# One hybrid decoder layer on one core: an earlier load of decay sums, two more PSUM banks for output chunks, gate samples by pairs of heads, and a tail that uses TensorE in place of GpSimd

## The chip, the cores and the metric

The kernel runs as one launch on one core of a Trainium2 chip. The metric is the device time of one execution in microseconds (us). A core has TensorE for matrix products (PE in the profile; PEld is its loading of weights, which runs beside the products), VectorE (DVE), ScalarE (ACT), GpSimd (POOL), and SyncE (SP), which here only starts transfers. Transfers (DMA) are started from the instruction queue of SP, ACT or POOL, and a queue runs its instructions in order.

## The reference

One decoder layer for 256 prompt tokens and 64 sample tokens (8 sequences of 8), 320 in all, in float32. Model width 2048, gate width 2048 in 16 heads of 128, state-space part (SSD) 2048 wide in 32 heads of 64 and 4 groups, state 128, FFN width 5632.

```python
h = rms_norm(x)
a_u, a_v, z, xbc, dt = split(h @ w_in)
# gate: per head, 128-token chunks; samples are 8 tokens each
v = layer_norm(gelu(a_v));  s = tril(w_s[head]) @ v[chunk, head] + b_s
gate_out = gelu(a_u) * s
# SSD: conv + silu on xbc, then per group g of 8 heads
da_cs = cumsum(dt * a)
decay = exp(tril(da_cs[t] - da_cs[s]))
y = (C B^T * decay) (dt x) + exp(da_cs) (C state) + d * x      # and the new states
ssm_out = group_rms_norm(y * silu(z))
x = x + rms_norm(concat(gate_out, ssm_out) @ w_out)
f = (gelu(conv(h2 @ w_up)[:, :5632]) * conv(h2 @ w_up)[:, 5632:]) @ w_down,  h2 = rms_norm(x)
y = x + rms_norm(f)
```

Outputs are y, the new SSD states, the last rows of the two convolutions, and v of the last gate chunk.

## The kernel before, in words

Activations lie with features on the 128 partitions and all 320 tokens in the free dimension. Each weight matrix comes in slabs of 128x1024 float32 (512 KB). `slab` (L100) starts the load of a slab on SP (`wraw`, L117), ACT rounds it to fp32r (`whi`, L123), and DVE subtracts (`wlo`, L124); each of the three tiles has three buffers. `accumulate` (L131) then makes three matmuls of 320 columns per 128x128 block: `whi` with the high part of the activation (L134), `whi` with its low part (L135) and `wlo` with the high part (L136). A slab so needs its `whi` for the first product of a block and its `wlo` for the third.

PSUM has eight banks here. Four belong to the pool `mm`: results of `project` (columns of `w_in` or `w_ffn_up`, named `ps`) and of `chunk_out` (named `pd`: 512 rows of `w_out` or `w_down`, 16 blocks of 128 outputs, each added to `acc_mix` or `acc_ffn` by DVE at L247). The other four belong to the pool `misc`, for everything small. Both pools hand out their banks in turn.

The program is written as a chain of projections and output chunks, with generator tasks in between: every few slabs `tick` advances the task at the head of `bg` by one step. A step issues its instructions into the engines' queues at that place. The tile scheduler adds the waits, and may shift an instruction among those of its engine by priority, so the order on each engine is fixed before the run.

The places of the change:

- **Gate.** `layer_norm` (L772 ff) normalizes v by token, in `vt` (128 tokens x 3 token tiles x 2048; the third tile has the 64 samples on partitions 0 to 63, and the other half is set to zero). `gate_mix(g)` handles four heads in one step, or in two: for each head two matmuls for the prompt's two chunks (L806, 128 columns) and one for the samples (L807, 64 columns). The sample weights `wS` are made by DVE from `w8`. These products are plain float32: each stands as two records of TensorE in the profile.
- **SSD.** `ssd(g)` runs in 13 steps over the slabs around it. `load_sums(j)` (L898) loads `cs`, the running decay sums of a pair of heads j; `decays` (L1041 to L1051) makes the decay matrices in the same tile, and `products` (L1062) multiplies with them (`y_ps`), at steps 6 (pairs 0, 1) and 12 (pairs 2, 3). `cs` tiles come from a pool of three buffers, and the two halves of the fourth state, `st3` (L906), take two of the same buffers at the group's start. L877 loads the other states. At the end of a group SP stores `s` and `x` (L1118, L1119).
- **Chunks.** `chunk_out(w_out, 3)` to `chunk_out(w_out, 6)` (L1180 to L1200) each follow a projection whose last results go through a convolution (`heads_in`: `pad` from `ps` at L452 and L453 on DVE, then L457 on ACT and L459 on DVE) or through `z_evac`.
- **Tail.** After the last chunk the squares are summed by matmul (`tsum`, L1391 and L1394), and `rsqrt_by_root` (L274 to L281) gives one factor per token, `rs_r`. The result lies in `f_tok` as ten slices of 128x512 (ten groups of 32 tokens), the residual in `x_tok` the same way. `y = f * r + x` is made for seven slices by DVE in one instruction each (L1417), stored by SP, and for slices 2, 5 and 8 by ACT (L1410, times r) and POOL (L1412, plus x), stored by ACT.

`tc.issue_after(i)` holds an instruction behind i in the order.

Of the kernel before, what the change touches and what calls it, by code (L numbers as in the profile page):

```python
# [8 lines left out]
F32 = mybir.dt.float32  # L9
# [24 lines left out]
def hybrid_step(  # L34
# [199 lines left out]
    def chunk_out(w, ck, hi, lo, begins, done=None, rate=1, apart=False):  # L234

        for nb in range(KD):
            if nb % 2 == 0:
                wb = slab(rows_of(w, 4 * ck, 4, P * nb, 256))
            ps = mm.tile([P, 512], F32, tag="mm", name=f"pd_{ck}_{nb}")
            for k in range(4):  # L240
                made = accumulate(ps[:, :NT], wb(k, nb % 2), hi[:, k, :], lo[:, k, :], k == 0, k == 3)
            with first():
                if begins:
                    act.copy(acc[:, nb, :], ps[:, :NT])
                else:
                    for ts in parts_of(nb) if apart else (slice(0, NT),):
                        added_last[:] = [dve.tensor_tensor(out=acc[:, nb, ts], in0=acc[:, nb, ts], in1=ps[:, ts], op=ALU.add).ins]  # L247
# [184 lines left out]
    with ExitStack() as mctx:  # L432
# [158 lines left out]
        with tc.tile_pool(name="gp", bufs=1) as gp:  # L591
# [8 lines left out]
            wS = gp.tile([P, 4, NB, TS], F32, name="wS")  # L600
            pool.memset(wS[NS:], 0.0)
# [127 lines left out]
            pool.memset(vt[NS:, 2], 0.0)  # L729
# [55 lines left out]
            def gate_mix(g, uf, res):  # L785
                wT = gp.tile([P, 4, P], F32, tag="wT", name="wT", bufs=1)
                w8 = gp.tile([NS, 4, TS], F32, tag="w8", name="w8", bufs=1)
# [14 lines left out]
                for j in range(4):  # L802
                    fs = slice(512 * g + P * j, 512 * g + P * j + P)
                    ps = misc("sg")
                    for c in range(2):
                        pe.matmul(ps[:, P * c:P * c + P], vt[:, c, fs], wT[:, j, :], start=True, stop=True)  # L806
                    pe.matmul(ps[:, NP:NT], vt[:, 2, fs], wS[:, j].rearrange("p b t -> p (b t)"), start=True, stop=True)  # L807
                    s = tp.tile([P, NT], F32, tag="ev", name="s", bufs=2)
                    dve.tensor_tensor(out=s[:, :NP].rearrange("p (c t) -> p c t", c=2),
                                      in0=ps[:, :NP].rearrange("p (c t) -> p c t", c=2),  # L810
                                      in1=bs[:, j, :].unsqueeze(1).to_broadcast([P, 2, P]), op=ALU.add)
                    dve.tensor_tensor(out=s[:, NP:].rearrange("p (b t) -> p b t", b=NB),
                                      in0=ps[:, NP:NT].rearrange("p (b t) -> p b t", b=NB),
                                      in1=bs[:, j, :TS].unsqueeze(1).to_broadcast([P, NB, TS]), op=ALU.add)
                    dve.tensor_tensor(out=s, in0=s, in1=uf[:, j, :], op=ALU.mult)
                    split(hi[:, j, :], lo[:, j, :], s)
                    if j % 2:
                        yield
# [35 lines left out]
        with tc.tile_pool(name="sd", bufs=1) as sd:  # L854
# [25 lines left out]
            sts_of = {g: [] for g in range(4)}  # L880
# [7 lines left out]
            def ssd(g):  # L888
# [15 lines left out]
                st3 = [sd.tile([P, 2, NT], F32, tag="cs", name="st3", bufs=3).rearrange("p i n -> p (i n)")[:, :512] for _ in range(2)]  # L904
                for h in range(2):
                    sp.dma_start(st3[h], state_ssm[4 * h + 3, g])  # L906
                cs_of = {0: load_sums(0)}
# [174 lines left out]
                for n in range(13 - e):  # L1082
# [40 lines left out]
            def load_ends():  # L1123
                s1s = sd.tile([P, 3, 512], F32, tag="xdt", name="s1s", bufs=1)
                for g in range(3):
                    x1 = sd.tile([P, 2, NT], F32, tag="cs", name="x1s", bufs=3).rearrange("p i n -> p (i n)")[:, :512]
# [55 lines left out]
            chunk_out(w_out, 3, hi, lo, False)  # L1182
# [3 lines left out]
            chunk_out(w_out, 4, *res[0], False)  # L1186
# [3 lines left out]
            chunk_out(w_out, 5, *res[1], False)  # L1190
# [3 lines left out]
            chunk_out(w_out, 6, *res[2], False)  # L1194
# [77 lines left out]
    with tc.tile_pool(name="fp", bufs=1) as fp:  # L1272
# [99 lines left out]
        BY_POOL = (2, 5, 8)  # L1372
# [35 lines left out]
        for c in BY_POOL:  # L1408
            with behind("act"):
                taken["act"] = act.activation(f[:, c], f[:, c], AF.Copy, scale=r[:, c:c + 1]).ins  # L1410
            with behind("pool"):
                taken["pool"] = pool.tensor_tensor(out=f[:, c], in0=f[:, c], in1=x[:, c], op=ALU.add).ins  # L1412
        for c in range(SN):
            if c in BY_POOL:
# [4 lines left out]
        for eng, queue in (("sp", sp), ("act", act)):  # L1419
            for c in range(SN):  # L1420
                if (c in BY_POOL) == (eng == "act"):
                    with behind(eng):
                        taken[eng] = queue.dma_start(o_y[:, c], f[:, c]).ins
# [11 lines left out]
def laid_out(a):  # L1435
# [7 lines left out]
    def states(v, n):  # L1443
# [19 lines left out]
        "gate_w8": np.concatenate([w8] * NB),  # L1463
# [43 lines left out]
```

## Time and profile before

| | before |
|---|---|
| median of 3 runs | 1756.57 us (1756.36 to 1757.76) |
| the profiled execution | 1756.8 us |
| its span in the trace | 1755.1 us |
| mean clock granted to TensorE | 0.997 |
| DMA, read and written | 280.51 MB and 19.69 MB, 171 GB/s over the span |

The span goes from the first to the last event in the trace. All times in the trace are us from its start. In lines of the timeline the first two numbers are the start and the length; several equal neighbours are put together (x4), and what stands in brackets at the end is the time for which the engine stood idle before, and what released it. SPq and ACTq are the queues that start transfers. TensorE's records overlap, since matmuls are pipelined: the distance from one start to the next says what a matmul costs, not its length.

### The profile page before, as it was taken

How to read it: one execution, taken by the hardware profiler on the slowest of the kernel's cores; microseconds unless marked ns; L12 is line 12 of the kernel's file. 1: busy time of each engine (PE TensorE's matmuls, PEld its weight loads, DVE VectorE, ACT ScalarE, POOL GpSimd, SP SyncE). 2: the span in 40 equal slices, each digit the busy share in tenths (PEclk: the TensorE clock that was granted, in tenths of full speed). 3: DMA queues.
4: the chain of work that ended last, by engine and by line, in shares of the span. 5: the costliest groups of instructions: out<-in, count | busy, mean ns of one | idle time of the engine just before them, and what ended most of it. 6: DMA issues, size and time to landing. Idle time of an engine off the chain costs nothing.

```text
span 1755.1 us, 31141 instructions
## 1 busy us (share of the span) xinstructions
PE 1738.4 (99%) x12079; PEld 1720.6 (98%) x12079; DVE 1181.1 (67%) x2015; ACT 820.0 (47%) x1199; POOL 328.5 (19%) x686
## 2 busy tenths in 40 slices
PE   9999999999999999999999999999999999999996
PEld 9999999999999999999999999999999999999996
DVE  6559864656969787778855566565657565656487
ACT  6344544334656565645544434343434343343435
POOL 2532330000423323112210101010202010101003
PEclk9999999999999999999999999999999999999998
DMA  7786565456566676665654545545454545454543
GB/s 241 240 235 177 180 177 155 154 161 194 190 210 202 214 220 190 213 197 162 187 157 146 156 148 154 150 148 156 151 153 148 156 149 150 153 154 148 152 152 108
DMA packets 227171, 302.24 MB, mean 172 GB/s; under 512 B 21328, under 2 KB 151504, under 8 KB 226832
## 3 DMA queue, kind: packets, MB, share of 16 engines
q1 hardware_dynamic: 210976, 272.42, 51.1%
q0 software_dynamic: 6176, 13.84, 2.6%
q10 hardware_dynamic: 9872, 14.00, 2.2%
q8 instruction: 95, 1.56, 0.4%
q14 instruction: 52, 0.43, 0.1%
HBM read 280.51 MB, written 19.69 MB: 171 GB/s over the span
## 4 chain that ended last, share of the span: by engine, by line
PE 60%; DVE 1%; issue 0%; DVEq 0%; ACT 0%
PE ps L134 13%; PE ps L135 12%; PE ps L136 12%; PE pd L134 7%; PE pd L136 7%; PE pd L135 7%; DVE f_tok L1417 0%; PE fin_ps L1134 0%; PE y_ps L1062 0%; PE ps_one L134 0%; PE ps_other L134 0%; PE ps_one L136 0%; PE ps_other L136 0%; PE ps_other L135 0%; PE ps_one L135 0%; PE ps L188 0%
## 5 line engine op out<-in xcount | busy, mean ns | idle before, releaser
L124 DVE TENSOR_TENSOR wlo<-wraw,whi 128x1024 fp32r<-128x1024 f32 (+2 forms) x480 | 583.5, 1216 | 426.3 <-ACT whi L123 424.1
L123 ACT CAST whi<-wraw 128x1024 fp32r<-128x1024 f32 (+2 forms) x479 | 495.8, 1035 | 677.0 <-PE ps L135 390.8
L134 PE MATMUL ps<-h_hi,whi 128*128 128x320 f32 x2428 | 750.3, 309 | 0.5 <-DVE acc_mix L247 0.5
L135 PE MATMUL ps<-h_lo,whi 128*128 128x320 f32 x2428 | 748.6, 308 | 0.0
L136 PE MATMUL ps<-h_hi,wlo 128*128 128x320 f32 x2428 | 748.0, 308 | 0.0
L134 PEld LDWEIGHTS ps<-h_hi,whi 128*128 128x128 f32 x2428 | 455.7, 188 | 3.8 <-issue 0.8
L135 PEld LDWEIGHTS ps<-h_lo,whi 128*128 128x128 f32 x2428 | 455.9, 188 | 0.4
L136 PEld LDWEIGHTS ps<-h_hi,wlo 128*128 128x128 f32 x2428 | 455.7, 188 | 0.0
L136 PE MATMUL pd<-fhi,wlo 128*128 128x320 f32 x704 | 217.0, 308 | 0.0
L134 PE MATMUL pd<-fhi,whi 128*128 128x320 f32 x704 | 217.0, 308 | 0.0
L135 PE MATMUL pd<-flo,whi 128*128 128x320 f32 x704 | 217.0, 308 | 0.0
L134 PE MATMUL pd<-ohi,whi 128*128 128x320 f32 x448 | 139.0, 310 | 1.7 <-DVE pad L453 1.7
L136 PE MATMUL pd<-ohi,wlo 128*128 128x320 f32 x448 | 138.3, 309 | 0.0
L135 PE MATMUL pd<-olo,whi 128*128 128x320 f32 x448 | 138.3, 309 | 0.0
L1308 POOL COPY ptf<-pad 128x2 f32<-128x2 f32 x88 | 21.1, 240 | 600.0 <-DVE pad L1296 599.3
L134 PEld LDWEIGHTS pd<-fhi,whi 128*128 128x128 f32 x704 | 132.2, 188 | 0.0
L135 PEld LDWEIGHTS pd<-flo,whi 128*128 128x128 f32 x704 | 132.2, 188 | 0.0
L136 PEld LDWEIGHTS pd<-fhi,wlo 128*128 128x128 f32 x704 | 132.2, 188 | 0.0
L247 DVE TENSOR_TENSOR acc_ffn<-acc_ffn,pd 128x320 f32<-128x320 f32 (+1 forms) x161 | 77.1, 479 | 29.5 <-PE pd L136 28.0
L134 PEld LDWEIGHTS pd<-ohi,whi 128*128 128x128 f32 x448 | 84.1, 188 | 3.0 <-issue 1.6
L135 PEld LDWEIGHTS pd<-olo,whi 128*128 128x128 f32 x448 | 84.1, 188 | 0.3
L136 PEld LDWEIGHTS pd<-ohi,wlo 128*128 128x128 f32 x448 | 84.1, 188 | 0.0
(339 smaller groups left out, 1737.2 us busy)
## 6 DMA issues: line engine op xcount, KB each, us to landing
wraw<-in_ffn_w_up SPq DMA_DIRECT2D x176, 512.0 KB, 3.7
wraw<-in_w_in SPq DMA_DIRECT2D x132, 512.0 KB, 3.8
wraw<-in_ffn_w_down SPq DMA_DIRECT2D x88, 512.0 KB, 3.4
wraw<-in_w_out SPq DMA_DIRECT2D x64, 512.0 KB, 3.4
st<-in_state_ssm SPq DMA_DIRECT2D x40, 256.0 KB, 4.6
out_ssm_state_sample<-st ACTq DMA_DIRECT2D x30, 256.0 KB, 2.7
cs<-dacs_d SPq DMA_DIRECT2D x16, 320.0 KB, 5.1
wraw<-in_w_in SPq DMA_DIRECT2D x12, 384.0 KB, 4.4
```

The lines of the kernel that those rows point to most:

```text
L123: rounded[:] = [act.copy(hi, raw).ins]
L124: dve.tensor_tensor(out=lo, in0=raw, in1=hi.bitcast(F32), op=ALU.subtract)
L134: pe.matmul(ps, whi, xhi, start=first, stop=False)
L135: pe.matmul(ps, whi, xlo, start=False, stop=False)
L136: last_made[0] = pe.matmul(ps, wlo, xhi, start=False, stop=last).ins
L247: added_last[:] = [dve.tensor_tensor(out=acc[:, nb, ts], in0=acc[:, nb, ts], in1=ps[:, ts], op=ALU.add).ins]
L1308: pool.tensor_copy(ptf[:, k, :], pad[:, 256:258])
```

## The change

Four edits, in one kernel:

1. **Gate.** The sample values of two heads lie one above the other: after a column block of the layer norm, four transfers from ACT's queue copy the odd heads' samples of `vt` from partitions 0 to 63 to partitions 64 to 127, next to those of the even heads. `wS` takes block form (128 x 2 pairs x 2 x 64), and one matmul of 128 columns gives the samples of two heads: 8 such matmuls in place of 16 of 64 columns. The setting to zero of half of `vt` by POOL goes, that of `wS` covers the whole tile.
2. **SSD.** The first decay sums of group g+1 are loaded at step 8 of group g (the ninth), and no longer at the start of group g+1. The three buffers of `cs` get fixed names so that this can be said: pair j of group g has buffer (g + j) mod 3, with j = 3 in the place of j = 0.
3. **Chunks.** `spare=2`: the first two results of the chunks 3 to 6 (`pd_0`, `pd_1`) take banks of `misc`.
4. **Tail.** Slices 3, 6 and 9 are made by TensorE and ACT: a matmul with the identity puts x into a PSUM bank (`both`) as soon as the sums are done, ACT multiplies f by r, a second matmul with the identity adds it to the bank, and ACT copies the bank out and stores it. POOL has no part in it.

```diff
-    def chunk_out(w, ck, hi, lo, begins, done=None, rate=1, apart=False):
+    def chunk_out(w, ck, hi, lo, begins, done=None, rate=1, apart=False, spare=0):
...
-            ps = mm.tile([P, 512], F32, tag="mm", name=f"pd_{ck}_{nb}")
+            ps = misc(f"pd_{ck}_{nb}") if nb < spare else mm.tile([P, 512], F32, tag="mm", name=f"pd_{ck}_{nb}")
...
-            wS = gp.tile([P, 4, NB, TS], F32, name="wS")
-            pool.memset(wS[NS:], 0.0)
+            wS = gp.tile([P, 2, 2, NB, TS], F32, name="wS")
+            pool.memset(wS, 0.0)
...
-            pool.memset(vt[NS:, 2], 0.0)
...
+                        if c == 2:
+                            upper_half, both_heads = (vt[rs, 2, 512 * q:512 * q + 512].rearrange("p (m i f) -> p m i f", m=2, i=2)
+                                                      for rs in (slice(NS, P), slice(0, NS)))
+                            act.dma_start(upper_half[:, :, 0], both_heads[:, :, 1])
...
-                        dve.tensor_tensor(out=wS[:NS, j], in0=w8[:, j].unsqueeze(1).to_broadcast([NS, NB, TS]),
-                                          in1=upper_s[:NS].rearrange("p (b t) -> p b t", b=NB), op=ALU.mult)
+                        rs = slice(NS * (j % 2), NS * (j % 2) + NS)
+                        dve.tensor_tensor(out=wS[rs, j // 2, j % 2], in0=w8[rs, j].unsqueeze(1).to_broadcast([NS, NB, TS]),
+                                          in1=upper_s[rs].rearrange("p (b t) -> p b t", b=NB), op=ALU.mult)
...
-                    for c in range(2):
-                        pe.matmul(ps[:, P * c:P * c + P], vt[:, c, fs], wT[:, j, :], start=True, stop=True)
-                    pe.matmul(ps[:, NP:NT], vt[:, 2, fs], wS[:, j].rearrange("p b t -> p (b t)"), start=True, stop=True)
...
+                        for c in range(2):
+                            pe.matmul(ps[:, P * c:P * c + P], vt[:, c, fs], wT[:, j, :], start=True, stop=True)
+                        if i == 0:
+                            pe.matmul(ps[:, NP:NP + P], vt[:, 2, fs], wS[:, m].rearrange("p i b t -> p (i b t)"), start=True, stop=True)
...
+            sts_of, first_sums = {g: [] for g in range(4)}, {}
...
-                def load_sums(j):
-
-                    cs = sd.tile([P, 2, NT], F32, tag="cs", name="cs", bufs=3)
+                def load_sums(j, g=g, h0=h0):
+
+                    cs = sd.tile([P, 2, NT], F32, tag=f"cs{(g + (j or 3)) % 3}", name="cs")
...
-                st3 = [sd.tile([P, 2, NT], F32, tag="cs", name="st3", bufs=3).rearrange("p i n -> p (i n)")[:, :512] for _ in range(2)]
+                st3 = [sd.tile([P, 2, NT], F32, tag=f"cs{(g + 1 + i) % 3}", name="st3").rearrange("p i n -> p (i n)")[:, :512] for i in range(2)]
...
-                cs_of = {0: load_sums(0)}
+                cs_of = {0: first_sums.pop(g) if g else load_sums(0)}
...
                         for j in decays_of.get(n, ()):
                             cs_of[j] = load_sums(j)
+                        if n == 8 and g < 3:
+                            first_sums[g + 1] = load_sums(0, g + 1, h0 + 8)
...
-            chunk_out(w_out, 4, *res[0], False)
+            chunk_out(w_out, 4, *res[0], False, spare=2)
...
-        BY_POOL = (2, 5, 8)
+        BY_SCALAR = (3, 6, 9)
...
-        for c in BY_POOL:
+        def scaled_by_root(c):
+
             with behind("act"):
                 taken["act"] = act.activation(f[:, c], f[:, c], AF.Copy, scale=r[:, c:c + 1]).ins
-            with behind("pool"):
-                taken["pool"] = pool.tensor_tensor(out=f[:, c], in0=f[:, c], in1=x[:, c], op=ALU.add).ins
+            with behind("pe"):
+                taken["pe"] = pe.matmul(both[c], ident, f[:, c], start=False, stop=True).ins
+
+        def taken_out(c):
+
+            with behind("act"):
+                taken["act"] = act.copy(f[:, c], both[c]).ins
+            with behind("act"):
+                taken["act"] = act.dma_start(o_y[:, c], f[:, c]).ins
+
+        both = {c: mm.tile([P, 512], F32, tag="mm", name="both") for c in BY_SCALAR}
+        taken["pe"] = made
+        for c in BY_SCALAR:
+            with behind("pe"):
+                taken["pe"] = pe.matmul(both[c], ident, x[:, c], start=True, stop=False).ins
+        a, b, d = BY_SCALAR
+        for step, c in ((scaled_by_root, a), (scaled_by_root, b), (taken_out, a), (scaled_by_root, d), (taken_out, b), (taken_out, d)):
+            step(c)
```

The number behind x in the following rows is that of equal neighbours, and `<-` stands between what an instruction writes and what it reads.

On TensorE, the gate's products of four heads (`sg`) behind the last block of an output chunk; before:

```order
L136 MATMUL pd_15_4502<-ohi,wlo 128x320
L806 MATMUL sg<-wT,vt 128x128 x2
L807 MATMUL sg<-wS,vt 128x64
L806 MATMUL sg<-wT,vt 128x128 x2
L807 MATMUL sg<-wS,vt 128x64
L806 MATMUL sg<-wT,vt 128x128 x2
L807 MATMUL sg<-wS,vt 128x64
L806 MATMUL sg<-wT,vt 128x128 x2
L807 MATMUL sg<-wS,vt 128x64
L134 MATMUL ps_0_4581<-h_hi,whi 128x320
```

and now:

```order
L136 MATMUL pd_15_4499<-ohi,wlo 128x320
L812 MATMUL sg<-wT,vt 128x128 x2
L814 MATMUL sg<-wS,vt 128x128
L812 MATMUL sg<-wT,vt 128x128 x4
L814 MATMUL sg<-wS,vt 128x128
L812 MATMUL sg<-wT,vt 128x128 x2
L134 MATMUL ps_0_4576<-h_hi,whi 128x320
```

The twelve products of four heads have become ten; the order around them is the same.

On SP's queue, the passage from SSD group 0 to group 1 (`st_...` are the halves of `st3`, `cs` the decay sums, `s_d` the store of group 0's `s`); before:

```order
L117 DMA wraw<-in_w_in 128x2x512
L906 DMA st_5609<-in_state_ssm 128x512
L117 DMA wraw<-in_w_in 128x2x512
L877 DMA st<-in_state_ssm 128x512 x2
L117 DMA wraw<-in_w_in 128x4x256 x2
L117 DMA wraw<-in_w_in 128x2x512
L877 DMA st<-in_state_ssm 128x512 x2
L117 DMA wraw<-in_w_in 128x2x512
L906 DMA st_5610<-in_state_ssm 128x512
L898 DMA cs<-dacs_d 128x2x320
L117 DMA wraw<-in_w_in 128x2x512
L1118 DMA s_d_99<-s_4823 128x512
```

and now:

```order
L117 DMA wraw<-in_w_in 128x2x512
L906 DMA cs<-dacs_d 128x2x320
L117 DMA wraw<-in_w_in 128x2x512
L885 DMA st<-in_state_ssm 128x512 x2
L117 DMA wraw<-in_w_in 128x4x256 x2
L117 DMA wraw<-in_w_in 128x2x512
L885 DMA st<-in_state_ssm 128x512 x2
L117 DMA wraw<-in_w_in 128x2x512
L914 DMA st_5606<-in_state_ssm 128x512
L914 DMA st_5607<-in_state_ssm 128x512
L1128 DMA s_d_99<-s_4818 128x512
L117 DMA wraw<-in_w_in 128x2x512 x4
```

The first half of `st3` and the decay sums have changed places, and one weight load that stood ahead of the store of `s` now stands behind it.

On ACT, the end of the program behind the square root (L277); now:

```order
L277 ACTIVATE rs_s<-rs_v 128x10
L1421 ACTIVATE f_tok<-f_tok,rs_r 128x512 x2
L1428 COPY f_tok<-both 128x512
L1430 DMA out_y<-f_tok 128x512
L1421 ACTIVATE f_tok<-f_tok,rs_r 128x512
L1428 COPY f_tok<-both 128x512
L1430 DMA out_y<-f_tok 128x512
L1428 COPY f_tok<-both 128x512
L1430 DMA out_y<-f_tok 128x512
```

Before, three multiplications (L1410) and three stores (L1423) stood there. TensorE, which ended with `tsum`, has six more matmuls of 128x512 behind it: three with x, three with f.

More of the change, by code (lines that the diff above doesn't have):

```diff
@@ L801, in gate_mix @@
                 res += hi, lo
-                for j in range(4):
-                    fs = slice(512 * g + P * j, 512 * g + P * j + P)
-                    ps = misc("sg")
-                    for c in range(2):
[L806 to L818, printed above, removed]
@@ new lines, in gate_mix @@
+                for m in range(2):
+                    both = [misc("sg") for _ in range(2)]
+                    for i, ps in enumerate(both):
+                        j = 2 * m + i
+                        fs = slice(512 * g + P * j, 512 * g + P * j + P)
+                        for c in range(2):
+                            pe.matmul(ps[:, P * c:P * c + P], vt[:, c, fs], wT[:, j, :], start=True, stop=True)
+                        if i == 0:
+                            pe.matmul(ps[:, NP:NP + P], vt[:, 2, fs], wS[:, m].rearrange("p i b t -> p (i b t)"), start=True, stop=True)
+                    for i, ps in enumerate(both):
+                        j = 2 * m + i
+                        s = tp.tile([P, NT], F32, tag="ev", name="s", bufs=2)
+                        dve.tensor_tensor(out=s[:, :NP].rearrange("p (c t) -> p c t", c=2),
+                                          in0=ps[:, :NP].rearrange("p (c t) -> p c t", c=2),
+                                          in1=bs[:, j, :].unsqueeze(1).to_broadcast([P, 2, P]), op=ALU.add)
+                        dve.tensor_tensor(out=s[:, NP:].rearrange("p (b t) -> p b t", b=NB),
+                                          in0=both[0][:, NP + NS * i:NP + NS * i + NS].rearrange("p (b t) -> p b t", b=NB),
+                                          in1=bs[:, j, :TS].unsqueeze(1).to_broadcast([P, NB, TS]), op=ALU.add)
+                        dve.tensor_tensor(out=s, in0=s, in1=uf[:, j, :], op=ALU.mult)
+                        split(hi[:, j, :], lo[:, j, :], s)
+                    yield
@@ L878, in load_state @@
                 return st
-            sts_of = {g: [] for g in range(4)}
+            sts_of, first_sums = {g: [] for g in range(4)}, {}
             def by_head(ap):
@@ L1125, in load_ends @@
                 for g in range(3):
-                    x1 = sd.tile([P, 2, NT], F32, tag="cs", name="x1s", bufs=3).rearrange("p i n -> p (i n)")[:, :512]
+                    x1 = sd.tile([P, 2, NT], F32, tag=f"cs{g}", name="x1s").rearrange("p i n -> p (i n)")[:, :512]
                     sp.dma_start(x1, x1_d[g])
@@ L1181, in hybrid_step @@
             heads_in_next(1)
-            chunk_out(w_out, 3, hi, lo, False)
+            chunk_out(w_out, 3, hi, lo, False, spare=2)
             norm = heads_out(0)
@@ L1189, in hybrid_step @@
             finish(norm)
-            chunk_out(w_out, 5, *res[1], False)
+            chunk_out(w_out, 5, *res[1], False, spare=2)
             norm = heads_out(2)
@@ L1193, in hybrid_step @@
             finish(norm)
-            chunk_out(w_out, 6, *res[2], False)
+            chunk_out(w_out, 6, *res[2], False, spare=2)
             finish(norm3)
@@ L1418, in hybrid_step @@
                                                         op0=ALU.mult, op1=ALU.add).ins
[L1419 to L1423, printed above, removed]
+        for c in range(SN):
+            if c not in BY_SCALAR:
+                with behind("sp"):
+                    taken["sp"] = sp.dma_start(o_y[:, c], f[:, c]).ins
 _OUTS = [
```

6 lines of the change are left out of this document (3 added, 3 removed).

## The prediction

> **What bounds the kernel now.** I read first the busy times of the page, then what TensorE waits for over the whole run.
>
> ```profile
> PE 1738.4 (99%) x12079; PEld 1720.6 (98%) x12079; DVE 1181.1 (67%) x2015; ACT 820.0 (47%) x1199; POOL 328.5 (19%) x686
> PE pd L134 <- DVE pad L453: 1.7, 2, 1.4
> ...
> PE ps L134 <- DVE acc_mix L247: 0.5, 1, 0.5
> ```
>
> TensorE is busy for 1738.4 of the span's 1755.1 us, and its named waits come to little more than 2 us (columns: us in total, times, longest). So there are only three places to win at: fewer products, the few waits of TensorE, and the stretch behind its last product, where it does nothing. The change touches all three. Everything on other engines is worth only what TensorE waits for it, except in the tail. Each wait is looked up below in the timeline, at its place; the excess is the distance between two starts less the ordinary one. The ordinary one is 0.14 to 0.15 us (548.11 to 548.25 in the second part's rows).
>
> **Gate: 16 products of 64 columns become 8 of 128.** Each stands as two records, so 32 records become 16. The rows are the weight loads of two heads, then the products.
>
> ```profile
> 416.01 0.53 PEld L806 LDWEIGHTS sg<-wT,vt 128*128 128x128 f32 x4
> 416.46 0.30 PEld L807 LDWEIGHTS sg<-wS,vt 128*128 128x128 f32 x2
> 416.68 0.53 PEld L806 LDWEIGHTS sg<-wT,vt 128*128 128x128 f32 x4
> ...
> 416.57 0.33 PE L807 MATMUL sg<-wS,vt 128*128 128x64 f32 x2
> 416.74 0.66 PE L806 MATMUL sg<-wT,vt 128*128 128x128 f32 x4
> ```
>
> Six weight loads of a head take 416.68 - 416.01 = 0.67 us. The four for products of 128 columns take 0.45, the two for products of 64 columns 0.22: both 0.11 us each. Weights are always 128x128, and they are loaded back to back, so they set the pace, whichever width the product has. A product of 128 columns keeps that pace (the four of them do). Sixteen records less are 16 x 0.112 = 1.8 us.
>
> The other bound: if the products' own columns set the pace, nothing is won, since 8 x 128 columns are as many as 16 x 64. For that speaks that the two records of 64 columns, read by the products' starts (416.57 to 416.74), take 0.17, that is 0.085 each and not 0.11. But the start of the next record is then late by as much, since its weights aren't there. I take 1.8 and keep 0 as a bound. The Trainium skill ("TensorE: Matmul & The Clock Gate", section "Back-to-back issue gap") gives the isolated gap of a matmul as about 60 cycles up to 64 columns and 134 cycles at 128, at 2.4 GHz: by it 32 x 25 ns = 0.80 us stand against 16 x 56 ns = 0.89, and the part would win nothing. The same section says that in a stream weight loads and products together set the spacing, and with that the rows above agree.
>
> The four transfers that copy the odd heads' samples stand in ACT's queue behind steps of the layer norm, so roundings may wait there for DVE; I cost it at nothing, since TensorE has no wait in its list for that stretch, and up to 1 us if that cover is thin. Setting `vt` to zero on POOL was on no path.
>
> **Spare banks: the starts of chunks 3 and 4.** TensorE at both, and DVE at chunk 4:
>
> ```profile
> 457.01 0.31 PE L136 MATMUL pd<-ohi,wlo 128*128 128x320 f32 x1
> 457.39 0.39 PE L134 MATMUL pd<-ohi,whi 128*128 128x320 f32 x1
> ...
> 548.11 0.31 PE L135 MATMUL ps<-h_lo,whi 128*128 128x320 f32 x1
> 548.25 0.31 PE L136 MATMUL ps<-h_hi,wlo 128*128 128x320 f32 x1
> 549.97 0.39 PE L134 MATMUL pd<-ohi,whi 128*128 128x320 f32 x1 [1.41 <-DVE pad L453]
> ...
> 550.34 0.31 PE L136 MATMUL pd<-ohi,wlo 128*128 128x320 f32 x1
> ...
> 555.20 0.31 PE L136 MATMUL pd<-ohi,wlo 128*128 128x320 f32 x1
> 555.76 0.39 PE L134 MATMUL pd<-ohi,whi 128*128 128x320 f32 x1 [0.25 <-DVE pad L453]
> ...
> 547.27 2.08 DVE L124 TENSOR_TENSOR wlo<-wraw,whi 128x1024 fp32r<-128x1024 f32 x1
> ...
> 549.61 0.21 DVE L453 TENSOR_TENSOR pad<-ps,r 128x64 f32<-128x64 f32 x1
> ```
>
> At 548.25 the projection's last product starts; the chunk's first block waits until DVE has emptied the first bank of the projection (549.61 + 0.21) and starts at 549.97: 1.72 less 0.15, an excess of 1.57. With a bank of `misc` the first two products can start at once, at about 548.40 and 548.55. What is late next is the subtraction of the very slab that the block needs: it ends at 547.27 + 2.08 = 549.35, and the third product reads it. So that product starts at about 549.45 and not at 550.34: the gain is about 0.87. The second wait, 555.20 to 555.76, has an excess of 0.41, and its bank is free too; I count it in full. Together 1.28. If the subtraction moves behind the emptying of another bank, the first gain is lost and 0.41 is left; if DVE reaches it sooner, both waits go, 1.57 + 0.41 = 1.98. At chunk 3 the excess is 457.39 - 457.01 - 0.15 = 0.23, and I count it as gone (0 as the other bound). Two blocks of a chunk hold banks of `misc` for a few us each; an SSD or gate task that gets such a bank next would have to come within these few us to wait, and none of TensorE's present waits is for a bank of `misc`. I count nothing for that.
>
> **First decay sums: a stall in the passage to group 3.** SP's two loads, ACT, DVE and TensorE:
>
> ```profile
> 639.59 0.46 SPq L906 DMA_DIRECT2D st<-in_state_ssm  x1
> ...
> 672.57 0.38 SPq L898 DMA_DIRECT2D cs<-dacs_d  x1
> ...
> 677.91 1.28 ACT L1041 ACT_TABLE_LOAD   x1 [6.14 <-DMA cs<-dacs_d]
> ...
> 680.60 1.92 DVE L124 TENSOR_TENSOR wlo<-wraw,whi 128x1024 fp32r<-128x1024 f32 x1 [2.26 <-ACT whi L123]
> ...
> 684.15 0.47 DVE L247 TENSOR_TENSOR acc_mix<-acc_mix,pd 128x320 f32<-128x320 f32 x1
> ...
> 683.90 0.31 PE L136 MATMUL ps<-h_hi,wlo 128*128 128x320 f32 x1
> 684.67 0.41 PE L134 MATMUL ps<-h_hi,whi 128*128 128x320 f32 x1 [0.47 <-DVE acc_mix L247]
> ```
>
> ACT stands for 6.14 us for the sums asked for at 672.57; behind it in its queue is the rounding of a slab, for that DVE stands 2.26 us, and with DVE late, the bank of a finished block is emptied late (684.15) and TensorE loses 684.67 - 683.90 - 0.15 = 0.62. The order of SP puts the sums into the place of the first half of `st3`, 639.59: 33 us earlier. Then ACT doesn't wait, DVE is up to 2.26 us earlier, and the 0.62 go. I count 0.6, with 0 as the other bound (ACT's next wait could stand there instead). ACT has such waits at the other groups' starts too, but TensorE shows no wait behind them.
>
> What is moved back: the first half of `st3` is loaded next to the second, which was already the later one, so nobody gets both later than now. One weight load per group now stands behind the store of `s`:
>
> ```profile
> 505.45 0.34 SPq L1118 DMA_DIRECT2D s_d<-s  x1
> ...
> 517.41 1.04 ACT L123 CAST whi<-wraw 128x1024 fp32r<-128x1024 f32 x1
> ```
>
> It is issued at about 505.8, and its slab is rounded at 517.41, nearly 12 us later: nothing. In group 0 the first sums shift by one weight load, on the same ground nothing, and up to 1 us lost if ACT's wait there grows.
>
> **Tail.** Three stretches of the windows, from the first stores to the end (columns: us, busy time of PE, PEld, DVE, ACT, POOL, clock, DMA share, GB/s), then DVE's and POOL's work and three prices.
>
> ```profile
> 1744.60:1745.40 0.80, 0.00 (x0) 0.00 (x0) 0.80 (x2) 0.80 (x2) 0.80 (x1) 1.00 0.01 3
> 1745.40:1753.40 8.00, 0.00 (x0) 0.00 (x0) 6.12 (x5) 0.31 (x1) 4.24 (x3) 0.55 0.88 328
> 1753.40:1754.40 1.00, 0.00 (x0) 0.00 (x0) 0.00 (x0) 0.00 (x0) 0.00 (x0) 0.50 0.00 0
> ...
> 1743.77 7.75 DVE L1417 SCALAR_TENSOR_TENSOR f_tok<-f_tok,rs_r,x_tok 128x512 f32<-128x512 f32 x7
> ...
> L1417 DVE SCALAR_TENSOR_TENSOR f_tok<-f_tok,rs_r,x_tok x7: 739/752/1755, 1743.8 to 1750.8; 128x512 f32<-128x512 f32 x7
> ...
> 1744.57 5.08 POOL L1412 TENSOR_TENSOR f_tok<-f_tok,x_tok 128x512 f32<-128x512 f32 x3 [7.00 <-ACT f_tok L1410]
> ...
> L1410 ACT ACTIVATE f_tok<-f_tok,rs_r x3: 707/707/722, 1743.8 to 1745.0; 128x512 f32<-128x512 f32 x3
> ...
> L1026 ACT COPY s<-s_ps x4: 578/581/582, 440.1 to 687.6; 128x512 f32<-128x512 f32 x4
> ...
> L1134 PE MATMUL fin_ps<-x1s,btok x6: 592/592/595, 806.4 to 808.9; 128*128 128x512 f32 x6
> ```
>
> DVE's seven slices take 7.75 us; one takes 0.74 to 0.75 in most cases and up to 1.755 while POOL adds, from 1744.57 to 1749.65. Without POOL they take at most 7 x 0.75 = 5.3, so DVE ends 2.5 us earlier or more. But the stores don't follow: ten of 256 KB are 0.88 x 8.00 = 7.04 us of all DMA engines at full share, and the first data moves at 1745.40 as before. They end at 1752.44 at the earliest, not 1753.40: a gain of 0.96, which I take as 1.0; the bounds are 0 and 2.5. The Trainium skill ("HBM Reference", section "Specifications (TRN2)") has a core that streams alone at about 425 GB/s: ten stores would then take 6.17 us, and the gain would be 1.8. The rows here give 328 / 0.88 = 373 GB/s at full share, and I go by them.
>
> The new way of three slices must keep ahead of that: ACT multiplies f three times at 0.71 us and copies three times at 0.58; TensorE adds f in two records of 0.59 at most for each slice, with x already in the banks. From 1743.8 the last copy so ends at about 1743.8 + 3 x 0.7 + 3 x 0.6 + one wait of 1.2 = 1748.9, and its store moves data from about 1750, while the queue drains until 1752.4. Some 2 us of cover: nothing, and one for one beyond it.
>
> **The sum.** 1.8 + 1.28 + 0.23 + 0.6 + 1.0 = 4.9 us, against the profiled execution's 1756.8: 1751.9. That execution stands 0.2 above the median of 1756.57, so the forecast is 1751.7.
>
> **Rivals.** A difference of 0.2%, 3.5 us, is about what a measurement of this kernel can tell from no change; below 1753.1 is faster, above 1760.1 slower.
>
> - The gate's products are paced by columns. For it: the starts 0.17 apart for two of 64 columns. Against: the weight loads' even 0.11. Gain 4.9 - 1.8 = 3.1, time 1753.5: no difference. 9 in 100.
> - The waits change their names: at 548 the subtraction keeps TensorE to the end (0.41 of 1.28 left), and at 684 another wait holds ACT or the copies of the gate hold it earlier (0 of 0.6). Gain 1.8 + 0.41 + 0.23 + 1.0 = 3.4, time 1753.1 and up: no difference. For it: DVE is the late one at both places, with work queued. 10 in 100.
> - Slower. The early sums may stand in SP's queue until their buffer is free, with the weight loads behind them. They take the buffer of pair 1. If that were not free before the group's last products (the rows below show when those free a buffer), the next weight load would go from 489.09 to behind 503.60.
>
> ```profile
> 489.09 0.37 SPq L117 DMA_DIRECT2D wraw<-in_w_in  x1
> ...
> 495.89 1.22 DVE L124 TENSOR_TENSOR wlo<-wraw,whi 128x1024 fp32r<-128x1024 f32 x1
> ...
> 503.49 0.41 PE L134 MATMUL ps<-h_hi,whi 128*128 128x320 f32 x1
> 503.60 0.38 SPq L898 DMA_DIRECT2D cs<-dacs_d  x1
> ```
>
> Its slab is ready 8.0 us after the load (495.89 + 1.22 - 489.09) and used at 503.49; issued at 504 it is ready at 512, 8.5 us late, at three passages 25 us: 1756.6 - 4.9 + 25, about 1777. It decides from 6.4 us of lateness of that load (503.49 - 497.11). Against it: pair 1 is multiplied in the group's step 6, two steps ahead of the load. 8 in 100.
>
> That a part doesn't do what it says, as with a slice of the tail that ends behind the stores, costs at most its own term, and is in the first two.
>
> **Chances.** My forecast, with its bounds a gain of 3.6 to 6.5: 70 in 100; the rivals 9, 10 and 8; still more gain 3. Faster 0.73, no difference 0.19, slower 0.08. The range goes from 1750.0, with 548 won in full (0.7 more) and the tail at somewhat over 1.0, to 1754.5, which takes in the first two rivals and 1 us lost on ACT.
>
> **What would show it.** Right: per head pair ten loads at 0.11 in the gate; the block at 548 starting its first product at once and its third at about 549.45; ACT without a wait for `cs` at 678, TensorE without one at 684; DVE's slices all at 0.75, and the windows behind 1740 with a DMA share near 1 to the end. Wrong: a TensorE wait on a slab around 503, 588 or 673; a wait for a `misc` bank behind a chunk's start; the last store issued after the others have landed; a gate block as long as before.

## The result and the profile after

| | before | after |
|---|---|---|
| median | 1756.59 us (6 runs, 1755.48 to 1757.76) | 1750.74 us (6 runs, 1750.20 to 1751.53) |
| ratio, 95% interval | | 0.9966 (0.9955 to 0.9976) |
| profiled execution, its span | 1756.8, 1755.1 us | 1750.2, 1748.5 us |

The change is 5.85 us faster; 4.9 were forecast. The head of the page after, and all that TensorE waits for by name (us in total, times, longest):

```profile
span 1748.5 us, 31128 instructions
...
PE 1740.9 (100%) x12075; PEld 1720.8 (98%) x12075; DVE 1181.3 (68%) x2015; ACT 822.2 (47%) x1202; POOL 316.8 (18%) x682
...
PE early L69 <- DVE ones L65: 1.1, 1, 1.1
PE both L1423 <- ACT f_tok L1421: 1.0, 1, 1.0
```

The waits for `pad` and `acc_mix` are gone from the list; the one that is new lies in the tail. Where the time went is read best from the starts of the same TensorE instructions in both traces (the first of each kind or group):

| start of | before | after | gain in the stretch | forecast |
|---|---|---|---|---|
| `dt` products | 48.77 | 48.42 | 0.34 | none |
| first `s_ps` (behind the gate) | 438.39 | 436.24 | 1.81 | 1.8 |
| second `s_ps` (chunk 3) | 520.38 | 517.96 | 0.27 | 0.23 |
| third `s_ps` (chunk 4) | 600.64 | 596.08 | 2.15 | 1.28 |
| fourth `s_ps` (passage to group 3) | 686.53 | 681.23 | 0.73 | 0.6 |
| `tsum` | 1740.24 | 1735.00 | -0.06 | 0 |
| end of the span | 1755.10 | 1748.46 | 1.39 | 1.0 |

Differences are of unrounded starts. The first stretch isn't the change's: among the traces of this study that start lies between 48.09 and 49.00 us. The other six add up to 6.3 us in this pair of traces. Three stretches also differ between traces of kernels whose code there is the same. With the code of before, the passage to group 3 is up to 1.35 us longer than in the trace of before, and the excess at chunk 3 goes from 0 to 0.5 us; the long stretch up to `tsum` differs by up to 0.8 us. So the 0.27 at chunk 3 can't be told from scatter.

The gate after, by its weight loads, for four heads:

```profile
413.61 0.56 PEld L812 LDWEIGHTS sg<-wT,vt 128*128 128x128 f32 x4
414.09 0.30 PEld L814 LDWEIGHTS sg<-wS,vt 128*128 128x128 f32 x2
414.31 0.97 PEld L812 LDWEIGHTS sg<-wT,vt 128*128 128x128 f32 x8
415.20 0.30 PEld L814 LDWEIGHTS sg<-wS,vt 128*128 128x128 f32 x2
415.43 0.53 PEld L812 LDWEIGHTS sg<-wT,vt 128*128 128x128 f32 x4
415.88 0.19 PEld L134 LDWEIGHTS ps<-h_hi,whi 128*128 128x128 f32 x1
```

Twenty loads take 415.88 - 413.61 = 2.27 us, 0.113 each, though two products in ten now have twice the columns.

The start of chunk 4 after, TensorE and then VectorE:

```profile
545.84 0.31 PE L136 MATMUL ps<-h_hi,wlo 128*128 128x320 f32 x1
545.99 0.31 PE L134 MATMUL pd<-ohi,whi 128*128 128x320 f32 x1
546.13 0.31 PE L135 MATMUL pd<-olo,whi 128*128 128x320 f32 x1
546.28 0.31 PE L136 MATMUL pd<-ohi,wlo 128*128 128x320 f32 x1
...
541.14 1.94 DVE L400 SCALAR_TENSOR_TENSOR olo<-xs,prm,ohi 128x320 fp32r<-128x320 f32 x4
542.99 1.22 DVE L124 TENSOR_TENSOR wlo<-wraw,whi 128x1024 fp32r<-128x1024 f32 x1
```

No wait at all, not even for the subtraction: it takes 1.22 us and not 2.08, the four L400 before it 1.94 and not 2.73, and it ends at 544.21, two us before the third product wants it. Why is found below.

The early sums after, on SP and on ACT:

```profile
478.67 0.42 SPq L885 DMA_DIRECT2D st<-in_state_ssm  x1
479.18 0.39 SPq L117 DMA_DIRECT2D wraw<-in_w_in  x1
479.66 0.42 SPq L906 DMA_DIRECT2D cs<-dacs_d  x1
...
667.22 1.28 ACT L1049 ACT_TABLE_LOAD   x1
668.51 0.42 ACT L1049 ACTIVATE cpx<-cs 128x256 f32<-128x256 f32 x1
```

SP issues the load at 479.66, right behind the weight load ahead of it: its buffer was free, and it held nothing up. In group 3, ACT starts on the sums without a wait, 10.7 us earlier than before; 4.6 of that had been won ahead of this stretch, and the other 6.1 are the wait.

The tail after: two stretches of the windows (us, busy PE, PEld, DVE, ACT, POOL, clock, DMA share, GB/s), of which the second goes from the first data of the stores to the last, and VectorE's slices.

```profile
1740.20:1746.20 6.00, 2.15 (x5) 0.49 (x3) 2.99 (x5) 2.36 (x4) 0.00 (x0) 1.00 1.03 381
1740.09:1747.15 7.06, 2.26 (x5) 0.49 (x3) 3.10 (x5) 2.36 (x4) 0.00 (x0) 0.94 1.00 371
...
1738.46 4.72 DVE L1444 SCALAR_TENSOR_TENSOR f_tok<-f_tok,rs_r,x_tok 128x512 f32<-128x512 f32 x7
```

VectorE needs 4.72 us in place of 7.75, and the DMA engines work at full share from the first data to the last: 7.06 us at 371 GB/s, where the same stretch of before took 8.01 us. (A share above 1 in a shorter stretch counts packets that begin in it and end behind it; 381 GB/s at 1.03 is the same rate.)

### The profile page after: what moved, and what is told of

It reads as the page before. It is cut to its first block, busy times and chain, and to the rows that moved or that the text cites. A ratio compares the mean times of both kernels' runs of the same rounds, so it can differ in the third digit from the quotient of the medians.

```text
span 1748.5 us, 31128 instructions
## 1 busy us (share of the span) xinstructions
PE 1740.9 (100%) x12075; PEld 1720.8 (98%) x12075; DVE 1181.3 (68%) x2015; ACT 822.2 (47%) x1202; POOL 316.8 (18%) x682
## 4 chain that ended last, share of the span: by engine, by line
PE 98%; DVE 1%; ACT 1%; issue 0%; POOLq 0%; ACTq 0%
PE ps L134 21%; PE ps L135 20%; PE ps L136 20%; PE pd L134 10%; PE pd L136 10%; PE pd L135 10%; PE y_ps L1070 1%; PE ps_v L135 1%; PE ps_v L134 1%; PE ps_v L136 1%; PE yo_ps L989 0%; PE up_ps L1006 0%; PE sg L812 0%; PE xt_ps L412 0%; DVE wlo L124 0%; ACT whi L123 0%
```

## The experiments

Times are medians, each beside the kernel before in the same series. That kernel scatters by itself over 1754.0 to 1758.3 us in 33 runs of one series, so differences under 1 us are read from the traces, stretch by stretch as in the table above. There is one trace of each kernel. The change's median of 1750.74 is of the first series; the kernel before stood at 1756.59 there and at 1756.40 to 1757.01 in the others, so a difference from 1750.74 is good to about half a us.

### Each part alone

The four edits of the change, one at a time on the kernel before. The gate alone:

> Only the gate's part of the change (samples of two heads in one matmul of 128 columns). Theory 1, weight loads set the pace: 16 records less at 0.112 us, 1.8 us faster than before, and the gate's block of four heads takes 20 x 0.112 = 2.2 us instead of 2.7. Theory 2, the products' columns set it: no gain, the block stays at 2.7 us. Everything else in the trace as before, the waits at 548 and 684 too.

Measured: 1755.47 against 1756.40 (0.9993, 0.9984 to 1.0002). The gate's stretch is 1.82 us shorter, and then 2.09 us are given back at chunk 3, which had an excess of 0.23 before; at chunk 4, where TensorE so comes later, the stretch is 0.98 us shorter than before. TensorE and VectorE at chunk 3, and VectorE's row of before behind them:

```profile
449.61 0.31 PE L136 MATMUL ps<-h_hi,wlo 128*128 128x320 f32 x1
450.91 0.39 PE L134 MATMUL pd<-ohi,whi 128*128 128x320 f32 x1 [0.99 <-DVE pad L453]
...
456.13 0.31 PE L136 MATMUL pd<-ohi,wlo 128*128 128x320 f32 x1
457.41 0.39 PE L134 MATMUL pd<-ohi,whi 128*128 128x320 f32 x1 [0.97 <-DVE pad L453]
...
450.55 0.21 DVE L453 TENSOR_TENSOR pad<-ps,r 128x64 f32<-128x64 f32 x1
...
451.18 0.21 DVE L453 TENSOR_TENSOR pad<-ps,r 128x64 f32<-128x64 f32 x1
```

Counted from the `dt` products, TensorE comes 1.8 us earlier and VectorE only 0.3: it has emptied the first bank of the projection at 450.76, before at 451.39, and the chunk waits for it twice. Theory 1 holds for the gate's block; that everything else stays as before was wrong.

> Only the two banks of misc for the first two results of chunks 3 to 6. Theory 1 (the prediction): the slab's subtraction is late next, DVE's order and its slow operations before it are unchanged, the third product starts at about 549.45; 1.3 us at 548 and 555 and 0.2 at 457, together 1.5 us faster. Theory 2 (both waits go by the banks alone): the third product at about 548.7, 2.0 + 0.2 = 2.2 us faster.

Measured: 1754.99 (0.9993, 0.9984 to 1.0002). In the trace 2.15 us at chunk 4 and 0.36 at chunk 3: theory 2 by its size. VectorE is quick at chunk 4, though nothing was done to it, and the wait would be gone there without the banks too. So this run doesn't say what the banks do at that place, as the next one shows.

> Only the early load of the next group's first decay sums. Theory 1 (the prediction): the stall at 684 goes, 0.6 to 0.7 us faster, the wait at 548 is as long as before, since it hangs on the landing of the norm's sums at 535. Theory 2: the group's start runs earlier on ACT and DVE, the norm's sums are stored and land earlier too (535 becomes 532), DVE comes to the subtraction of the slab earlier, and the wait at 548 shrinks as well: 1.5 to 2.5 us faster in all. Theory 3, the slower one: weight loads stand behind the early load in SP's queue, 20 us slower.

Measured: 1754.48 (0.9991, 0.9983 to 1.0000). The passage to group 3 is 0.73 us shorter, as forecast, and no weight load is late. But chunk 4 is 2.12 us shorter too, without any spare bank. Theory 2's size is right, its reason doesn't hold. VectorE has the norm's sums at 534.03 here, 1.2 us earlier than before and not 3; it has them at 533.91 with the spare banks alone, and at 534.16 with the gate alone, where VectorE is as slow at chunk 4 as before. Two different edits go with the end of the same wait, and the earlier sums don't explain it.

> Only the new tail (TensorE and ACT for three slices, nothing on GpSimd). Theory 1, the stores bound the tail: DVE's slices end 3 us earlier, the last data lands 1.0 to 1.4 us earlier, DMA share near 1 from the first data to the last; 1.0 to 1.4 us faster. Theory 2, the adding bounds it: 2.5 to 3 us faster.

Measured: 1755.83 (0.9996, 0.9987 to 1.0005). Behind `tsum` 1.06 us less: theory 1. Ahead of it, where the code is that of before, this trace is 1.55 us slower, 1.35 of it in the passage to group 3: TensorE waits there twice for `acc_mix`, and not once. Those waits differ from trace to trace.

### What makes the wait at chunk 4

GpSimd's rows explain it. At this place it multiplies the fourth state by its decay (L992), in two instructions, as soon as that state has landed; VectorE has four L400 and the slab's subtraction there. GpSimd's first instruction and the fourth L400 in the kernel before:

```profile
545.85 1.16 POOL L992 TENSOR_TENSOR st<-st,tote 128x512 f32<-128x512 f32 x1 [13.91 <-DMA st<-in_state_ssm]
...
546.00 1.35 DVE L400 SCALAR_TENSOR_TENSOR olo<-xs,prm,ohi 128x320 fp32r<-128x320 f32 x1
```

and with the spare banks alone, with the subtraction behind:

```profile
544.72 0.55 DVE L400 SCALAR_TENSOR_TENSOR olo<-xs,prm,ohi 128x320 fp32r<-128x320 f32 x1
...
545.18 1.23 DVE L124 TENSOR_TENSOR wlo<-wraw,whi 128x1024 fp32r<-128x1024 f32 x1
...
544.82 2.51 POOL L992 TENSOR_TENSOR st<-st,tote 128x512 f32<-128x512 f32 x1 [13.99 <-DVE olo L400]
```

In the one, GpSimd starts 0.15 us ahead: it takes 1.16 us, the L400 1.35 and not 0.55, and the subtraction behind it, beside GpSimd's second instruction, 2.08 and not 1.23. In the other, the L400 starts 0.10 us ahead: VectorE runs at its own speed, and GpSimd's first takes 2.51. Whoever starts first goes through, and the other stands; VectorE so goes through with two instructions in a row, since GpSimd's first ends at 547.33, 0.92 us behind the end of the subtraction. The Trainium skill ("SBUF — State Buffer", section "SBUF: two separate sides") has this as an exclusive lock on a pair of ports that VectorE and GpSimd share, held for a whole instruction by the one that starts first. With that the first rows agree: the L400 ends at 547.35, 0.34 us behind GpSimd's first instruction. The second rows go further, since there the turn passes from the L400 to the subtraction and not to GpSimd.

So a quarter of a microsecond between a landing DMA and VectorE's queue decides 1.65 us on VectorE, and with them the wait. That GpSimd is the cause was tested on the kernel before, by leaving out GpSimd's multiplication of each group's fourth state (whose results are then not decayed):

```diff
-                    if n in shrinks:
+                    if n in shrinks and n != 8:
```

> The kernel before, with the multiplication of each group's fourth state by its decay on GpSimd (L992, at step 8) left out, and nothing else changed. Theory 1, the wait at 548 is made by GpSimd and VectorE at the same time: the four L400 take 1.94 us and not 2.73, the subtraction behind them 1.2 and not 2.1, DVE empties the banks 1.65 us earlier, and both waits at 548 and 555 are gone with the banks as before: 2.1 us faster there. Theory 2, DVE is late there for its own queue: the wait stays at 1.5 us.

TensorE and VectorE:

```profile
547.99 0.31 PE L136 MATMUL ps<-h_hi,wlo 128*128 128x320 f32 x1
548.14 0.31 PE L134 MATMUL pd<-ohi,whi 128*128 128x320 f32 x1
...
544.23 1.94 DVE L400 SCALAR_TENSOR_TENSOR olo<-xs,prm,ohi 128x320 fp32r<-128x320 f32 x4
546.09 1.22 DVE L124 TENSOR_TENSOR wlo<-wraw,whi 128x1024 fp32r<-128x1024 f32 x1
```

Theory 1: the first wait is gone with the banks as before, 1.78 us in that stretch (of the second wait 0.30 is left). The median is 1755.26 against 1756.73 (0.9995, 0.9986 to 1.0004). The wait was GpSimd's.

What puts one of them ahead stays open. Thirteen traces have GpSimd's work there. VectorE's last L400 was slow in all four that have neither the spare banks nor the early sums; of the nine that have either or both, it was slow in one (the run without the gate, below). So it doesn't look like mere scatter, but no run here shows by which way these two edits do it, and with one trace of each kernel a single case proves little: in three of the traces GpSimd and an L400 start within 0.02 us of each other.

### Each part left out of the change

> The change without its spare banks (gate, early sums and tail stay). Theory 1, the banks are cover for the gate's gain: at chunk 3 DVE empties the projection's banks at the same time as in the change, TensorE arrives there 1.8 us early and waits, as in the kernel with the gate's part alone (2.1 us there); at 548 no wait, since the early sums alone took it away. About 2 us slower than the change, 1752.5 to 1753. Theory 2 (the prediction: the banks are worth 1.5, nearly all at 548): 1.5 us slower, with the waits at 546 and none at 449.

Measured: 1752.31 (0.9975, 0.9966 to 0.9985), 1.57 above the change's 1750.74. Theory 1: TensorE waits twice at chunk 3 and not at chunk 4, where VectorE was first again (us in total, times, longest):

```profile
PE pd L134 <- DVE pad L453: 1.3, 2, 1.0
```

The stretch of chunk 3 is 1.47 us longer than before and so 1.73 longer than in the change.

> The change without the early sums (gate, spare banks and tail stay). Theory 1: only the stall at the passage to group 3 comes back, 0.6 to 1.4 us, since the banks alone cover chunk 3 and 4: 1751.4 to 1752.2. Theory 2: DVE late at 548 as well (its slow subtraction comes back, 0.9 us more): up to 1753.

Measured: 1751.51 (0.9970, 0.9959 to 0.9982), 0.8 above. Theory 1: chunks 3 and 4 as in the change, and one wait of TensorE, for `acc_mix`, in the passage to group 3; that stretch is 1.0 us longer than in the change.

> The change without the gate's part. With the spare banks there, the gate's gain is not given back at chunk 3: 1.75 us slower than the change, 1752.5. If the banks only hide it in part, less than that.

Measured: 1752.65 (0.9975, 0.9965 to 0.9984), 1.9 above. The gate's stretch is 1.80 us longer and nothing is given back behind it. Here VectorE lost to GpSimd at chunk 4:

```profile
543.69 2.75 POOL L992 TENSOR_TENSOR st<-st,tote 128x512 f32<-128x512 f32 x2 [12.45 <-DMA st<-in_state_ssm]
...
542.78 2.74 DVE L400 SCALAR_TENSOR_TENSOR olo<-xs,prm,ohi 128x320 fp32r<-128x320 f32 x4
545.44 2.08 DVE L124 TENSOR_TENSOR wlo<-wraw,whi 128x1024 fp32r<-128x1024 f32 x1
...
547.44 0.31 PE L136 MATMUL ps<-h_hi,wlo 128*128 128x320 f32 x1
547.59 0.31 PE L134 MATMUL pd<-ohi,whi 128*128 128x320 f32 x1
547.74 0.31 PE L135 MATMUL pd<-olo,whi 128*128 128x320 f32 x1
547.88 0.31 PE L136 MATMUL pd<-ohi,wlo 128*128 128x320 f32 x1
```

And TensorE doesn't wait: the bank is spare, and the subtraction ends at 547.52, 0.36 us before the third product. This is the case that the prediction had in mind, and here the banks do spare TensorE a wait at chunk 4: about 0.5 us by estimate, since the projection's first bank is empty only at 547.99. The third product isn't late, though, since VectorE begins its L400 4.8 us ahead of the chunk and would have begun 3.8 ahead before. What put it further ahead wasn't tried.

> The change with the tail of before. Behind the last product 1.1 to 1.4 us longer than the change, nothing else: 1752.0. If the sums of the parts are all independent, the other three parts alone are 4.5 us faster than before.

Measured: 1752.24 (0.9974, 0.9964 to 0.9985), 1.5 above; behind `tsum` 1.31 us longer than the change. The other three parts together are 4.8 us faster than before.

### What paces the gate, and what bounds the tail

```diff
-                    pe.matmul(ps[:, NP:NT], vt[:, 2, fs], wS[:, j].rearrange("p b t -> p (b t)"), start=True, stop=True)
+                    jw = min(j, 2)
+                    pe.matmul(ps[:, NP:NP + P], vt[:, 2, fs], wS[:, jw:jw + 2].rearrange("p j b t -> p (j b t)"), start=True, stop=True)
...
```

> The kernel before, with each head's sample product made 128 columns wide in place of 64 (the other 64 columns are those of a neighbouring head and aren't read); still 16 products. Theory 1, weight loads set the pace: the block of four heads takes the same 2.7 us as before, no change in time. Theory 2, the columns set it: 32 records x 0.055 = 1.8 us longer in all.

```profile
415.71 0.53 PEld L806 LDWEIGHTS sg<-wT,vt 128*128 128x128 f32 x4
416.16 0.30 PEld L808 LDWEIGHTS sg<-wS,vt 128*128 128x128 f32 x2
416.38 0.53 PEld L806 LDWEIGHTS sg<-wT,vt 128*128 128x128 f32 x4
```

A head takes 0.67 us, as with half the columns, and the stretch of the gate differs by 0.01: theory 1. (The median is 1756.09, 0.6 below its kernel before: 0.9996, 0.9987 to 1.0004, which shows how little such medians can tell.)

Two tails on the change, with its other three parts. In the first, ten slices on VectorE, made from the tail of before by one line:

```diff
-        BY_POOL = (2, 5, 8)
+        BY_POOL = ()
```

> The change with another tail: all ten slices on VectorE in one instruction each, ten stores by SP, nothing on TensorE, ScalarE or GpSimd. VectorE ends 2.0 us later than in the change (ten slices 0.67 us apart and not seven). Theory 1, the stores bound the tail: ten slices 0.67 apart come hardly slower than ten stores can go (0.65 to 0.70 each), so the end is 0.2 to 0.5 us later than the change's. Theory 2, the adding bounds it: 2 us later.

```profile
1739.36 6.72 DVE L1427 SCALAR_TENSOR_TENSOR f_tok<-f_tok,rs_r,x_tok 128x512 f32<-128x512 f32 x10
...
1741.10:1747.50 6.40, 0.00 (x0) 0.00 (x0) 4.97 (x8) 0.00 (x0) 0.00 (x0) 0.50 1.02 381
```

Measured: 1749.84 (0.9961, 0.9949 to 0.9974). Behind `tsum` it takes 13.40 us, the change 13.46, the kernel before 14.86, and the change with the tail of before, from which this kernel differs in that line alone, 14.77. VectorE works 2.0 us longer than in the change, and the stores go at the same 381 GB/s: theory 1, and without even the few tenths that it allowed for. VectorE alone makes a slice every 0.66 us, and the ten stores take 0.70 each. The way over TensorE and ScalarE isn't what won the time; that GpSimd left VectorE alone did. The interval overlaps with the change's, so the times don't tell the two apart, and this one has less in it.

In the second, the first slice is made and stored in two halves:

```diff
-            with behind("dve"):
-                taken["dve"] = dve.scalar_tensor_tensor(out=f[:, c], in0=f[:, c], scalar=r[:, c:c + 1], in1=x[:, c],
+            for fs in (slice(0, 256), slice(256, 512)) if c == 0 else (slice(0, 512),):
+                with behind("dve"):
+                    taken["dve"] = dve.scalar_tensor_tensor(out=f[:, c, fs], in0=f[:, c, fs], scalar=r[:, c:c + 1], in1=x[:, c, fs],
...
```

> The change, with the first slice of the tail made and stored in two halves of 256 columns. Theory 1, the stores bound the tail from their first data on: the first data moves 0.3 us earlier and the end comes 0.2 to 0.3 us earlier. Theory 2, something behind bounds it (the last store on ScalarE's queue): no gain.

Measured: 1750.35 (0.9963, 0.9951 to 0.9976), and 13.46 us behind `tsum`: nothing won. The first store was issued 0.26 us earlier, counted from `rs_r`, but the six us behind it moved at a share of 0.97 and not 1.03, 356 GB/s. The second row is a piece of them:

```profile
1740.00:1746.00 6.00, 2.51 (x6) 0.68 (x4) 3.48 (x6) 2.36 (x4) 0.00 (x0) 1.00 0.97 356
1740.85:1741.10 0.25, 0.25 (x2) 0.00 (x0) 0.25 (x1) 0.25 (x1) 0.00 (x0) 1.00 0.40 131
```

The DMA engines ran dry. At 1740.9 both halves are through, and the data of the second slice doesn't move yet: VectorE makes that slice no earlier than in the change, but 0.1 us later, counted from `rs_r`, since two halves take it longer than a whole slice. So the stores bound the tail only as long as the next slice is ready, which the change and the kernel with VectorE alone just manage. Theory 1 missed here, and theory 2's store on ScalarE's queue isn't needed to explain it.

## Why the prediction was right, point by point

- **Gate, 1.8.** Right in size and mechanism: 1.8 in every trace with this part, and the width made no difference. The rival by columns is out. The isolated gap of the Trainium skill ("TensorE: Matmul & The Clock Gate", section "Back-to-back issue gap") is no price for this block; its sentence on a stream of loads and products fits. Missing was that the gain is given back at chunk 3 unless the banks are there: the prediction costed the parts as if TensorE's coming earlier changed nothing behind it. That the sum held all the same is luck: the change's own second part covered it.
- **Spare banks, 1.28 and 0.23.** The term that was mis-sized: 2.15 at chunk 4. The step that failed is "What is late next is the subtraction of the very slab that the block needs: it ends at 547.27 + 2.08". The 2.08 was taken as the operation's own time, though its ordinary length is 1.22; it was long, and the L400 before it, because GpSimd was at work beside them (1.94 and 1.22 without it). The prediction had read just that in the tail's rows. And the banks' worth isn't where it was put: without them the change loses 1.73 at chunk 3 and nothing at chunk 4. The 0.27 at chunk 3 fits the 0.23 by luck, since the excess there is anything from 0 to 0.5 in traces without the gate's part and the banks.
- **First sums, 0.6.** Right: 0.73 in the change and alone, and ACT's wait is gone. The stretch is equally long in every trace with this part; without it, it is 0.7 to 2.1 us longer, so the trace of before shows the part at nearly its least. The slower rival is out: the load went out without a wait at 479.66.
- **Tail, 1.0.** Right that the stores bound it, and the term is right nearly to the digit: from first data to last they take 7.06 us, where 7.04 were forecast, 0.95 less than before. Of the 1.39 us behind `tsum`, another 0.07 lie ahead of the first data, and 0.37 behind the last: from there to the end of the span it is 1.69 us before, 1.31 in the change, and 1.60 with the change's tail alone. So that piece differs with the same tail, and what makes it wasn't tried. The 425 GB/s of the Trainium skill ("HBM Reference", section "Specifications (TRN2)") weren't reached. That TensorE's way must keep ahead was right and beside the point, since VectorE alone does as well.
- **The second rival** (waits change their names) stayed out because VectorE was first or far enough ahead at chunk 4 in every trace with early sums.
- **The forecast** of 1751.7 is 1.0 above the measured time. In the traces the terms sum to 6.3 and not 4.9: the wait at chunk 4 was 0.9 too small, and the tail 0.4, for what lies outside its stores.

## What to carry to other kernels

An operation that takes nearly twice its ordinary time in a trace may be waiting and not working, as both did here: before its length goes into a sum, look at what ran beside it, and who started first. Gains ahead of a wait don't add up by themselves; ask for each place behind whether the engine that TensorE waits for there comes earlier too. Here one part (the banks) is the cover of another (the gate), so the gate is worth less alone; and two parts each go with the end of the same wait, so that wait is counted twice when they are measured alone. The sum of the parts alone, 4.8 us by medians against 5.85 together, hides this: the two errors have opposite signs, and each of these medians is uncertain by more than 1 us.

## What the runs showed of the hardware

- VectorE and GpSimd: with starts 0.10 to 0.15 us apart, the later one stands: 1.35 in place of 0.54 us for a 128x320 operation of VectorE, which ends 0.34 us behind GpSimd's, or 2.51 in place of 1.06 for a 128x512 one of GpSimd, which ends 0.92 us behind the second of two operations of VectorE. Which of them is first differs between traces whose instructions at this place are the same.
- A float32 product with fresh 128x128 weights costs 0.11 us per record at 64 and at 128 columns alike.
- Ten stores of 256 KB took 7.06 us from first data to last (371 GB/s) from two queues, with three engines making the slices, and 7.03 us (373 GB/s) from one queue, with VectorE alone.
